# Four moves in the order of a diffusion layer: two at the opening, one in the first modulation pairs, one at the start of the second FFN

## The chip, the cores and the metric

The kernel runs on one core of a Trainium2 chip. The metric is the device time of one execution in microseconds (us). Engines are named as the profile names them: PE (matrix multiplications; PEld is its weight load), DVE (vector), ACT (activation and copies with scale), POOL, and SP, which here only issues DMA transfers. A queue of an engine is shown as SPq, POOLq and so on.

## The reference, cut to what matters

One layer, float32, on 256 latent tokens `x` and 256 context tokens `ctx`, each 2048 wide:

```python
mod_l = (silu_c @ w_mod[l] + b_mod[l]).reshape(B, N_MOD, D_MODEL)
mod_c = (silu_cc @ w_mod[l] + b_mod[l]).reshape(1, N_MOD, D_MODEL)
xl = half_step_ffn(xl, mod_l, 0, g_norm[l, 0], w_ffn1_up[l], w_ffn1_down[l])
xc = half_step_ffn(xc, mod_c, 0, g_norm[l, 0], w_ffn1_up[l], w_ffn1_down[l])
...                                   # attention and mLSTM mix both sequences
xl = half_step_ffn(xl, mod_l, 6, g_norm[l, 2], w_ffn2_up[l], w_ffn2_down[l])
```

`half_step_ffn` normalises a token by its root mean square, multiplies by `1 + scale` and adds `shift` (two of the nine rows of the modulation), multiplies by `w_up` (2048 to 2 x 5632), forms `silu(a) * b`, multiplies by `w_down` and adds the gated result. The scale and shift of the first FFN (rows 1 and 0 of `w_mod`, 2 x 16 MB) have to be computed before its first multiplication; that is the opening of the kernel. The second FFN runs on the latent tokens alone.

## The kernel before, in words

Products in float32 are made of three float32r products: each operand is split into `hi` (ACT, line 126) and `lo` (DVE, line 127). Tokens stand transposed, as 16 column blocks `k` of 128 features by 512 tokens, in `hhi` and `hlo`.

**The opening** (lines 485 to 743, about the first 128 us) does four things at once. It loads the four token tiles `xs` (context 0 and 1, latent 0 and 1, 1 MB each). It computes the conditions: `cc`, a 16 KB tensor with both condition vectors, is loaded twice (as `cc`, and as `c8` in a tile called `hi`), goes through Silu on ACT, is transposed by PE into `cP`, and is spread over the 128 partitions by 16 matmuls with 8 rows (tile `cB`, lists `spread`). It normalises the token tiles (`squares`, `factor`, `normal`) and turns them with PE, 512 columns a group (`turned`; ACT copies each group back, line 556). And it streams the first two rows of `w_mod` in 32 units of 1 MB through four buffers `mraw` (`mod_unit`), plus parts of `w_up` for the first three column pairs of the hidden layer (`products`, loads `w_pre`). `idle(n)` issues n matmuls whose result nobody reads.

The two modulation rows are computed for blocks of columns (`BLOCKS`): one column block alone, seven pairs, one alone. For a pair there are four units of `w_mod`, in this order of loading; I call them **D** (shift of the pair's first column, summed by DVE against `cB`, twice 2.3 us), **A** (shift of its second column), **B** and **C** (scale of both columns, half the rows each). A, B and C are multiplied by PE with `cP` (`mod_sums`; in the profile `tr<-mraw,cP`, because the bank has the name `tr`). Between these sums PE works off the waiting products of the pair before (`steps(prods)`: six matmuls a step for a pair). After C the sums are transposed (`mod_turned`, `tr<-ident,row`), DVE and ACT form the scaled tokens (`pair_scaled`), and the rest of the old products (18 matmuls) is issued. The four token tiles have four groups each; two of each are turned at once (`N_FIRST`), the other eight by `turned_ahead`, one at a time between the sums: three in the first pair, three in the second, two in the third.

In this stretch vector, tensor and scalar instructions are pinned to the order in which the code issues them; SP's loads too (`tc.keep_in_program_order`). Later a scheduler orders what is not pinned. SP issues its transfers one after the other; a load whose buffer is not free holds up those behind it.

**The second FFN** (from line 2030 on) streams `w_up2` and `w_dn2` in units of 1 MB through five `raw` slots (`ask` issues a load, `next_split` takes the next loaded tile, splits it and asks for one more). Its first hidden block is a plain product (`up(1)`, called through `unit`), the others are `quad`s: products on quarter matrices whose weight tiles `chain2c` and `chain2r` are summed by accumulating DMAs. The tiles of the first quad are loaded by `first_tiles`: `chain2c`, two tiles, and later `chain2r`. Five loads are asked for ahead, each plain unit asks for one more, and `first_tiles(0, ...)` stands after the second plain unit.

Of the kernel before, what the change touches and what calls it, by code (L numbers as in the profile page):

```python
# [9 lines left out]
F32 = mybir.dt.float32  # L10
# [3 lines left out]
AF = mybir.ActivationFunctionType  # L14
# [5 lines left out]
P = 128  # L20
D = 2048
# [27 lines left out]
CTX, LAT = 0, 1  # L49
# [7 lines left out]
def tile_layer(ctx: ExitStack, tc: tile.TileContext, I: dict, out: bass.AP):  # L57
    nc = tc.nc
# [12 lines left out]
    def bank():  # L71
        return ps["mm"].tile([P, 512], F32, tag="mm", name="mm")

    def tbank():
        return ps["tr"].tile([P, 512], F32, tag="tr", name="tr")
# [136 lines left out]

    sm.tile([P, 16], F32, name="smpad", bufs=1)
    cc = sm.tile([32, P], F32, tag="gr", name="cc")
    tc.keep_in_program_order(nc.sync.dma_start(cc, I["cc"]))
    nc.scalar.activation(cc, cc, AF.Silu)
    SC = cst.tile([P, 3, 2, KT], F32, name="SC")
    SH = cst.tile([P, 3, 2, KT], F32, name="SH")
    cst.tile([P, 40], F32, name="cstpad")
# [5 lines left out]
    def conditions(cB, h0, h1, seqs=(CTX, LAT)):  # L225

        for s in seqs:
            nc.sync.dma_start(cB[s], ccd[s, h0 * 1024 : h1 * 1024].partition_broadcast(P))
# [12 lines left out]
    def scale_of(n, s, kk):  # L241

        vector[0].scalar_tensor_tensor(SC[:, n, s, kk], SC[:, n, s, kk], 1.0, gnT[:, n, kk], op0=ALU.add, op1=ALU.mult)
# [48 lines left out]
    class Beside:  # L292
# [49 lines left out]
        def steps(self):  # L342
            half = None
            while self.n < len(self.items) or self.due or self.late:
                while self.n < len(self.items):
                    h = self.items[self.n][2]
                    if h != half:
                        half = h
                        conditions({LAT: self.cB}, h, h + 1, (LAT,))
                        self.waits += WAIT  # L350
                    if self.n not in self.slots or self.done < np.interp(self.n, *zip((0, 0), *self.pace)) + self.waits:
                        break
                    self.one()
                yield
                self.done += 1
                for x in [x for x in self.due if x[0] <= self.done]:
                    self.due.remove(x)
                    self.finish(*x[1:])
                if self.late and self.late[0][0] <= self.done:
                    mod_rows_out(*self.late.pop(0)[1:])  # L360
# [17 lines left out]
    def mod_rows_out(i, s, v):  # L378

        pg = tbank()  # L380
        tc.keep_in_program_order(nc.tensor.transpose(pg[:KT, :P], v, ident))
        gr = sm.tile([KT, P], F32, tag="gr", name="gr")
        nc.vector.tensor_copy(gr, pg[:KT, :P])
        nc.sync.dma_start(mod_rows[i][s, :].rearrange("(k p) -> k p", p=P), gr)
# [91 lines left out]
    xsrc = {CTX: I["ctx"], LAT: I["x"]}  # L476
# [9 lines left out]
    pre = [[bank(), bank()] for _ in range(NPRE)]  # L486
    with pool(name="st", bufs=1) as st:
        scratch.append(st)
        cP = st.tile([P, KT, 32], F32, name="cP")
        nc.gpsimd.memset(cP, 0.0)  # L490
        xs0 = {}

        vector[0], tensor[0] = Pinned(nc.vector), Pinned(nc.tensor)
        still = wp.tile([P, 1024], F32R, tag="lo", name="lo", bufs=4)[:, :CB]
# [37 lines left out]
        def squares(s, t):  # L532

            ss = sm.tile([P, 4], F32, tag="ss4", name="ss4", bufs=4)[:, :2]
            x, n = xs0[s, t], 1280
            tc.keep_in_program_order(nc.scalar.activation(junka, x[:, :n], AF.Square, accum_out=ss[:, 0:1]))
            x = x[:, n:]
            vector[0].scalar_tensor_tensor(junk[:, : D - n], x, 1.0, x, op0=ALU.mult, op1=ALU.mult, accum_out=ss[:, 1:2])
            return ss
# [11 lines left out]
        def turned(s, t, g, b):  # L551

            x = xs0[s, t][:, g * CB : (g + 1) * CB]
            for j in range(4):
                tensor[0].transpose(b[:, j * P : (j + 1) * P], x[:, j * P : (j + 1) * P], ident)
            tc.keep_in_program_order(nc.scalar.activation(x, b, AF.Copy))

        def turned_ahead():

            for g in range(N_FIRST, NCB):  # L560
                for s in (CTX, LAT):
                    for t in range(2):
                        turned(s, t, g, tbank())
                        yield

        def columns(s, k0, k1):
# [32 lines left out]
        def mod_unit():  # L599
            if ready:  # L600
                return ready.pop(0)
            raw = st.tile([P, 2048], F32, tag="mraw", name="mraw", bufs=4)
            tc.keep_in_program_order(nc.sync.dma_start(raw, I["w_m0"][next(unit)]))
            return raw

        def mod_sums(i, k0, k1, last=iter(())):

            n = (k1 - k0) * P
            nk = 2048 // n
            b = tbank()[:, :n]  # L610
            for g in range(KT // nk):
                if g == KT // nk - 1:
                    steps(last)
                raw = mod_unit()
                for j in range(nk):
                    k = nk * g + j
                    q = 32 * (j % 4)
                    tensor[0].matmul(
                        b[q : q + 32, :], cP[:, k, :], raw[:, j * n : (j + 1) * n], start=k < 4, stop=k >= KT - 4, tile_position=(0, q), skip_group_check=True
                    )  # L620
                yield
            row = st.tile([P, 256], F32, tag="row", name="row", bufs=3)[:, :n]
            scalar[0].activation(row, b, AF.Copy)
            turns.append((i, k0, k1, row))
# [15 lines left out]

        turns = []

        xs2 = [st.tile([P, 2, D], F32, name=f"xs{s}") for s in (CTX, LAT)]
        for s in (CTX, LAT):
            for t in range(2):
                x = xs0[s, t] = xs2[s][:, t, :]
                tc.keep_in_program_order(nc.sync.dma_start(x, xsrc[s][t * P : (t + 1) * P, :]))
        tc.keep_in_program_order(nc.sync.dma_start(vecs, I["vecs"]))
        ready += [mod_unit(), mod_unit()]
        prods = products(1, pre, 0, 1, hhi, hlo, True)  # L650
# [26 lines left out]
        last = squares(*tiles[3])  # L677
# [17 lines left out]
        ahead = turned_ahead()  # L695
        for k0, k1 in BLOCKS[1:]:
            kk = slice(k0, k1)
            following = products(1, pre, k0, k1, hhi, hlo, middle=True)
            if k1 - k0 == 2:
                raw = mod_unit()  # L700
            for i in range(2):
                for n, _ in enumerate(mod_sums(i, k0 if i else k1 - 1, k1, following if i else iter(()))):
                    steps(prods, 3 - (k1 - k0))
                    if not n:
                        steps(ahead)
                if i:
                    steps(ahead)
                if not i and k1 - k0 == 2:
                    for s in (CTX, LAT):
                        vector[0].scalar_tensor_tensor(  # L710
                            junk.bitcast(FP8), raw, 1.0, cB[:, s, :], op0=ALU.mult, op1=ALU.mult, accum_out=SH[:, 0, s, k0 : k0 + 1], saturate=False
                        )
                    biased(0, k0, k0 + 1)

            if k0 != 1:
                steps(following)
            mod_turned()
            if k0 != 1:
                steps(prods)
            for s in (CTX, LAT):  # L720
                scale_of(0, s, kk)
            if k0 == 1:
                steps(following)
                steps(prods)
            if k1 - k0 == 1:
                x_scaled(k0)
            else:
                for s in (CTX, LAT):
                    pair_scaled(k0, s)
            drain(prods)  # L730
            prods = following
            if k0 == 1:
                scalar[0] = nc.scalar
            if k1 == KT:
                nc.sync.dma_start(ccd.rearrange("s (k p) -> (s k) p", p=P), cc)
# [565 lines left out]
    with ExitStack() as mx:  # L1301
# [197 lines left out]
        st = states()  # L1499
# [214 lines left out]
        k1 = one([P, 2, 2, T], "k1", F32R, tag="slot1")  # L1714
# [218 lines left out]
        for cb in range(NCB):  # L1933
            bs = []
            weave(out_proj(cb, (1,), bs), xT)
            if cb == NCB - 1:

                pre = [[bank()[:, : T + 2], bank()[:, : T + 2]] for _ in range(NPRE)]
                prods = products(2, pre, 0, 4, h2hi, h2lo, both=True)
# [26 lines left out]
        for q in range(NCB):  # L1966
            if q:
                prods = products(2, pre, 4 * q, 4 * q + 4, h2hi, h2lo)
# [10 lines left out]
    with f2x:  # L1979
# [54 lines left out]
        sets = [[f3.tile([P, 2048], F32, tag=f"{g}{q}", name=f"chain2{g}{q}") for q in range(2)] for g in "cr"]  # L2034
# [57 lines left out]
        def first_tiles(ab, c, tiles):  # L2092
            for q in range(2):
                pin(nc.sync.dma_start(tiles[q], part(QUADS[0], ab, c + q)))
# [251 lines left out]
        def unit(n=1):  # L2346
            for _ in range(n):
                next(plain_units)
                clock[0] += 2
                turned()  # L2350

        ask(nc.sync, N_RAW)
        for n in range(3):
            unit()
            if n == 1:
                first_tiles(0, 0, sets[0])
                steps(forms)
        for n in QUADS:
            for step, _ in enumerate(quad(n)):
# [172 lines left out]
```

## Time and profile before

| | us |
|---|---|
| median of 3 runs | 2596.65 (2595.49 to 2597.49) |
| the profiled execution: its own time | 2592.96 |
| its span in the trace | 2591.3 |
| PE busy in the span | 2568.9 (99%) |
| DVE busy | 2167.0 (84%) |
| ACT busy | 1442.8 (56%) |

The span runs from the first to the last instruction; 1.7 us of the execution's own time lie outside it, and this execution was 3.7 us below the median. In rows of the timeline the first number is the start in us from the span's start, the second how long the group lasted from its first start to its last end; in brackets stands how long the engine was idle before it, and what ended the wait. In rows of DMA issues the last number is the time from issue to landing.

### The profile page before, as it was taken

The numbers are of one execution on the slowest core, as the hardware profiler recorded it, in microseconds if no ns is written. First come the engines' busy times: TensorE is split into PE (matmuls) and PEld (weight loads), VectorE is DVE, ScalarE is ACT, GpSimd is POOL, SyncE is SP. The second block draws the span as 40 slices with busy tenths as digits, with TensorE's granted clock in tenths as the row PEclk, the third lists the DMA queues.
The fourth block names the chain that finished last, engine by engine and source line by source line (L and its number), as shares of the span: only waits on it lengthen the run. The fifth ranks groups of instructions, "written<-read, shape, count | busy, mean of one in ns | idle before, by whom it ended". The sixth has DMA issues, their size and how long they took to land.

```text
span 2591.3 us, 33902 instructions
## 1 busy us (share of the span) xinstructions
PE 2568.9 (99%) x12659; PEld 2142.3 (83%) x12659; DVE 2167.0 (84%) x2826; ACT 1442.8 (56%) x1877; POOL 262.4 (10%) x359
## 2 busy tenths in 40 slices
PE   8999999999999999999999999999999999999998
PEld 6688888888888888888889989888897888888887
DVE  6698888878888788888887888798888888888888
ACT  5454444444444465444454457467476767666664
POOL 0000000100000100000110000110001111111111
PEclk9999999999999999999999999999999999999999
DMA  9889999999999988889986887677768899999985
GB/s 390 344 226 274 269 284 273 257 278 285 257 292 263 279 248 240 214 218 226 228 258 256 299 289 244 236 267 263 262 219 279 266 274 272 269 277 272 275 259 187
DMA packets 127669, 684.72 MB, mean 264 GB/s; under 512 B 14208, under 2 KB 16768, under 8 KB 64912
## 3 DMA queue, kind: packets, MB, share of 16 engines
q0 software_dynamic: 42048, 284.18, 46.4%
q1 hardware_dynamic: 85456, 398.37, 41.4%
q8 instruction: 99, 1.62, 0.2%
q14 instruction: 66, 0.54, 0.1%
HBM read 664.60 MB, written 17.89 MB: 263 GB/s over the span
## 4 chain that ended last, share of the span: by engine, by line
PE 93%; DVE 2%; DMA 2%; ACT 1%; issue 1%; POOL 0%; ACTq 0%; POOLq 0%; SPq 0%; DVEq 0%
PE mm L172 54%; PE Y L172 7%; PE X L172 6%; PE mm L150 4%; PE mm L149 4%; PE mm L148 4%; PE mm L85 3%; PE tr L149 2%; PE tr L150 2%; PE tr L148 2%; PE tr L85 1%; DVE lo L127 1%; DMA mraw<-in_w_m 1%; PE tr L876 1%; PE mm L1755 1%
## 5 line engine op out<-in xcount | busy, mean ns | idle before, releaser
L126 ACT ACTIVATE hi<-raw 128x1024 fp32r<-128x1024 f32 (+3 forms) x490 | 499.4, 1036 | 356.3 <-PE mm L172 220.5
L127 DVE TENSOR_TENSOR lo<-raw,hi 128x1024 fp32r<-128x1024 f32 (+2 forms) x476 | 563.6, 1204 | 150.3 <-ACT hi L126 108.7
L172 PE MATMUL mm<-hi,hhi 128*128 128x512 f32 (+3 forms) x1024 | 391.2, 384 | 0.0
L172 PE MATMUL mm<-hi,hlo 128*128 128x512 f32 (+3 forms) x1024 | 385.0, 378 | 0.0
L126 ACT ACTIVATE hi<-chain 128x1024 fp32r<-128x1024 f32 x240 | 247.5, 1056 | 223.3 <-PE mm L172 102.2
L127 DVE TENSOR_TENSOR lo<-chain,hi 128x1024 fp32r<-128x1024 f32 x240 | 287.9, 1221 | 82.5 <-ACT hi L126 74.3
L172 PE MATMUL mm<-lo,hhi 128*128 128x512 f32 (+3 forms) x1024 | 253.6, 378 | 0.0
L233 DVE SCALAR_TENSOR_TENSOR junk<-sraw,cBh 128x1024 fp8e5<-128x1024 f32 x192 | 234.4, 1221 | 17.7 <-DMA sraw<-in_w_mt 15.3
L172 PEld LDWEIGHTS mm<-hi,hhi 128*128 128x128 f32 x1024 | 192.9, 188 | 31.4
L172 PEld LDWEIGHTS mm<-hi,hlo 128*128 128x128 f32 x1024 | 192.8, 188 | 31.0
L172 PEld LDWEIGHTS mm<-lo,hhi 128*128 128x128 f32 x1024 | 187.1, 188 | 33.0
L127 DVE TENSOR_TENSOR lo<-chain2c,hi 128x1024 fp32r<-128x1024 f32 x112 | 135.6, 1222 | 34.3 <-ACT hi L126 30.1
L126 ACT ACTIVATE hi<-chain2c 128x1024 fp32r<-128x1024 f32 x112 | 118.5, 1061 | 70.6 <-PE mm L172 47.4
L127 DVE TENSOR_TENSOR lo<-chain2r,hi 128x1024 fp32r<-128x1024 f32 x104 | 125.9, 1222 | 28.4 <-ACT hi L126 24.4
L126 ACT ACTIVATE hi<-chain2r 128x1024 fp32r<-128x1024 f32 x104 | 110.4, 1061 | 63.1 <-PE mm L172 45.1
L172 PE MATMUL mm<-lo,hid2h 128*128 128x512 f32 x352 | 137.3, 390 | 0.0
L172 PE MATMUL mm<-hi,hid2l 128*128 128x512 f32 x352 | 137.0, 390 | 0.0
L172 PE MATMUL mm<-hi,hid2h 128*128 128x512 f32 x352 | 135.8, 390 | 0.0
L777 POOL DMA_DIRECT2D chain<-in_w_up1b x60 | 52.6, 877 | 732.7 <-DVE lo L127 606.7
L233 DVE SCALAR_TENSOR_TENSOR sr<-sr,cBl 128x1024 f32<-128x1024 f32 x85 | 102.5, 1217 | 15.8 <-DMA sr<-in_w_mt 15.8
L172 PE MATMUL mm<-hhi,hi 128*128 128x512 f32 (+1 forms) x256 | 83.9, 347 | 0.0
L172 PE MATMUL mm<-hlo,hi 128*128 128x512 f32 (+1 forms) x256 | 81.3, 337 | 0.0
(519 smaller groups left out, 5751.8 us busy)
## 6 DMA issues: line engine op xcount, KB each, us to landing
chain<-in_w_up1b POOLq DMA_DIRECT2D x60, 1024.0 KB, 10.5
sraw<-in_w_mt SPq DMA_DIRECT2D x96, 512.0 KB, 8.0
raw<-in_w_dn POOLq DMA_DIRECT2D x48, 1024.0 KB, 12.6
chain2c<-in_w_up2b POOLq DMA_DIRECT2D x44, 1024.0 KB, 10.9
chain2r<-in_w_up2b POOLq DMA_DIRECT2D x42, 1024.0 KB, 9.8
sr<-in_w_mt SPq DMA_DIRECT2D x82, 512.0 KB, 5.5
raw<-in_w_up1b SPq DMA_DIRECT2D x40, 1024.0 KB, 8.5
mraw<-in_w_m SPq DMA_DIRECT2D x32, 1024.0 KB, 8.1
```

The lines of the kernel that those rows point to most:

```text
L85: ins = getattr(self.engine, name)(*a, **k)
L126: scalar[0].activation(hi, src, AF.Copy)
L127: vector[0].tensor_tensor(lo, src, hi.bitcast(F32), op=ALU.subtract)
L148: tensor[0].matmul(out_ap, sh, mh, start=first, stop=False, skip_group_check=skip)
L149: tensor[0].matmul(out_ap, sh, ml, start=False, stop=False, skip_group_check=skip)
L150: tensor[0].matmul(out_ap, sl, mh, start=False, stop=last, skip_group_check=skip)
L172: tensor[0].matmul(o, st_, mv, start=first, stop=last, skip_group_check=skip)
L233: ins = nc.vector.scalar_tensor_tensor(junk() if junk else raw, raw, 1.0, cB[s], op0=ALU.mult, op1=ALU.mult, accum_out=mT[:, i, s, kt, h : ...
L777: accum = lambda dst, src: nc.gpsimd.dma_start(dst, src, accum_op=ALU.add)
L876: nc.tensor.transpose(tb[:, j * P : (j + 1) * P], ca[:, j * P : (j + 1) * P], ident)
L1755: nc.tensor.matmul(o[t][:, g * P : (g + 1) * P], av[:, k, kv * HD : (kv + 1) * HD], p[:, k * P : (k + 1) * P], start=g == 0 and k == 0, st ...
```

## The change

Four things are edited.

1. `token_load`: the load of the first context tile is issued before the two loads of `cc`; the other three token tiles and everything else on SP follow as before. (The tile pair `xs2` is therefore allocated earlier.)
2. `turned_ahead` takes two banks (`unused`) that the first pair's products have not reached yet, for the second tile of each sequence in the first group row; and in the first pair it is stepped twice where it was stepped once. The first pair turns five groups, the second three, the third none.
3. `mod_sums(..., both)`: for the six pairs from column 3 on, units B and C are multiplied one right after the other, and the two steps of products that stood after B and after C follow together.
4. `first_tiles(0, ...)` of the second FFN is called after the first plain unit instead of the second.

```diff
-    tc.keep_in_program_order(nc.sync.dma_start(cc, I["cc"]))
-    nc.scalar.activation(cc, cc, AF.Silu)
...
+        token_load(CTX, 0)
+        tc.keep_in_program_order(nc.sync.dma_start(cc, I["cc"]))
+        tc.keep_in_program_order(nc.scalar.activation(cc, cc, AF.Silu))
...
+        unused = [pre[2][1], pre[2][0]]
...
-                        turned(s, t, g, tbank())
+                        turned(s, t, g, unused.pop() if unused and (s, t) in ((CTX, 1), (LAT, 1)) else tbank())
...
-                yield
+                if g or not both:
+                    yield
...
-                for n, _ in enumerate(mod_sums(i, k0 if i else k1 - 1, k1, following if i else iter(()))):
-                    steps(prods, 3 - (k1 - k0))
+                for n, _ in enumerate(mod_sums(i, k0 if i else k1 - 1, k1, following if i else iter(()), i and 2 < k0 < k1 - 1)):
+                    steps(prods, 2 if i and 2 < k0 < k1 - 1 else 3 - (k1 - k0))
                     if not n:
-                        steps(ahead)
+                        steps(ahead, 2 if k0 == 1 else 1)
...
             unit()
+            if n == 0:
+                first_tiles(0, 0, sets[0])
             if n == 1:
-                first_tiles(0, 0, sets[0])
                 steps(forms)
```

SP at the very beginning, before; `hi<-in_cc` is the load of `c8`:

```order
L215 DMA cc<-in_cc 32x128
L508 DMA hi<-in_cc 8x512
L647 DMA xs_159<-in_ctx 128x2048 x2
L647 DMA xs_160<-in_x 128x2048 x2
L648 DMA vecs<-in_vecs 128x296
L603 DMA mraw<-in_w_m 128x2048 x2
```

and with the change:

```order
L493 DMA xs_112<-in_ctx 128x2048
L496 DMA cc<-in_cc 32x128
L514 DMA hi<-in_cc 8x512
L493 DMA xs_112<-in_ctx 128x2048
L493 DMA xs_113<-in_x 128x2048 x2
L654 DMA vecs<-in_vecs 128x296
L611 DMA mraw<-in_w_m 128x2048 x2
```

The 16 KB loads now stand behind one megabyte; the rest keeps its order.

PE in one of the middle pairs, from the products after unit A on (`tr<-mraw,cP` are units B and C), as a difference:

```order
 L85 MATMUL mm<-hlo,hi 128x512 x2
-L85 MATMUL tr<-mraw,cP 32x256 x8
+L85 MATMUL tr<-mraw,cP 32x256 x16
 L85 MATMUL mm<-hhi,hi 128x512
 L85 MATMUL mm<-hhi,lo 128x512
 L85 MATMUL mm<-hhi,hi 128x512
 L85 MATMUL mm<-hhi,lo 128x512
 L85 MATMUL mm<-hlo,hi 128x512 x2
-L85 MATMUL tr<-mraw,cP 32x256 x8
 L85 MATMUL mm<-hhi,hi 128x512
```

Unit C moves up past six product matmuls; nothing else in the pair moves. On DVE no instruction changes its place in the whole program.

SP at the start of the second FFN, before (seven plain loads, then the two chained tiles) and with the change:

```order
L2081 DMA raw<-in_w_up2b 128x2048 x7
L2094 DMA chain2c_16095<-in_w_up2b 128x2048
L2094 DMA chain2c_16096<-in_w_up2b 128x2048
L2081 DMA raw<-in_w_up2b 128x2048
L2094 DMA chain2r_16097<-in_w_up2b 128x2048
```

```order
L2087 DMA raw<-in_w_up2b 128x2048 x6
L2100 DMA chain2c_16093<-in_w_up2b 128x2048
L2100 DMA chain2c_16094<-in_w_up2b 128x2048
L2087 DMA raw<-in_w_up2b 128x2048 x2
L2100 DMA chain2r_16095<-in_w_up2b 128x2048
```

The seventh plain load changes places with the two chained tiles; POOL's own DMAs keep their order.

More of the change, by code (lines that the diff above doesn't have):

```diff
@@ L490, in tile_layer, with token_load @@
         nc.gpsimd.memset(cP, 0.0)
-        xs0 = {}
+        xs2 = [st.tile([P, 2, D], F32, name=f"xs{s}") for s in (CTX, LAT)]
+        xs0 = {(s, t): xs2[s][:, t, :] for s in (CTX, LAT) for t in range(2)}
+        def token_load(s, t):
+            tc.keep_in_program_order(nc.sync.dma_start(xs0[s, t], xsrc[s][t * P : (t + 1) * P, :]))
+        token_load(CTX, 0)
+        tc.keep_in_program_order(nc.sync.dma_start(cc, I["cc"]))
+        tc.keep_in_program_order(nc.scalar.activation(cc, cc, AF.Silu))
         vector[0], tensor[0] = Pinned(nc.vector), Pinned(nc.tensor)
@@ L604, in mod_unit, with mod_sums @@
             return raw
-        def mod_sums(i, k0, k1, last=iter(())):
+        def mod_sums(i, k0, k1, last=iter(()), both=False):
             n = (k1 - k0) * P
@@ L641, in tile_layer @@
         turns = []
[L643 to L647, printed above, removed]
+        for s, t in ((CTX, 1), (LAT, 0), (LAT, 1)):
+            token_load(s, t)
         tc.keep_in_program_order(nc.sync.dma_start(vecs, I["vecs"]))
```

## The prediction

> **What bounds the kernel now.** First the page: is one engine busy all the time?
>
> ```profile
> span 2591.3 us, 33902 instructions
> PE 2568.9 (99%) x12659; PEld 2142.3 (83%) x12659; DVE 2167.0 (84%) x2826; ACT 1442.8 (56%) x1877; POOL 262.4 (10%) x359
> ```
>
> PE is idle for 22.4 us in all, so an edit can gain little except where those idle times lie. The edits touch the opening and the start of the second FFN. The opening by windows (from:to, length, busy us of PE, PEld, DVE, ACT, POOL, then granted PE clock, DMA share, GB/s):
>
> ```profile
> 10.00:20.00 10.00, 8.98 (x42) 6.36 (x45) 8.06 (x16) 7.33 (x13) 2.20 (x4) 0.68 1.02 427
> 53.37:66.52 13.15, 13.15 (x112) 9.46 (x112) 9.25 (x18) 6.38 (x12) 0.00 (x0) 1.00 0.94 367
> 66.52:78.77 12.25, 12.25 (x104) 8.47 (x103) 9.34 (x18) 5.19 (x10) 0.00 (x0) 1.00 0.97 359
> ```
>
> Early on the DMAs set the pace (427 GB/s, PE idle 1 us in ten); the last two rows are the third and fourth pair, from unit A to the next unit A, with PE full and the DMAs nearly so. Which of the two ends the opening is told by the chain of waits (start, us, what):
>
> ```profile
> 96.29 1.04 PE tr L85 x16
> ...
> 97.36 11.93 DMA mraw<-in_w_m
> ...
> 109.33 1.07 PE tr L85 x16
> 110.40 1.59 PE mm L85 x6
> ...
> 112.32 4.14 PE mm L85 x18
> 116.46 1.01 PE tr L85 x32
> 117.47 2.94 PE mm L85 x12
> ```
>
> The chain passes through a transfer: unit C of the seventh pair landed at 109.29 and PE had waited for it. From there PE runs without a gap to 123. So this landing is the anchor of the opening, and what PE saves ahead of it is lost in the wait unless the landing moves too.
>
> **First edit: the token tile first.** SP, ACT and PE at the beginning, then landings of single issues (the tile issued at 1.66, `vecs` issued at 3.62, unit B of the first pair issued at 20.9), then the range for all units:
>
> ```profile
> 0.80 0.40 SPq L215 DMA_DIRECT2D cc<-in_cc  x1
> 1.66 0.83 SPq L647 DMA_DIRECT2D xs<-in_ctx  x2
> 2.48 0.31 ACT L216 ACTIVATE cc<-cc 32x128 f32<-32x128 f32 x1 [0.41 <-DMA cc<-in_cc]
> 3.84 0.31 PE L85 MATMUL tr<-ident,cc 32*128 32x32 f32 x1
> 4.08 2.32 PE L85 MATMUL mm<-lo 128*128 128x512 f32 x5
> 6.33 4.49 PE L85 MATMUL mm<-lo,hi 8*128 8x512 f32 x16
> xs<-in_ctx SPq DMA_DIRECT2D x1, 1024.0 KB, 4.7
> vecs<-in_vecs SPq DMA_DIRECT2D x1, 148.0 KB, 10.6
> mraw<-in_w_m SPq DMA_DIRECT2D x1, 1024.0 KB, 7.6
> DMA to landing us min/median/max: 4.8/8.1/16.1
> ```
>
> `vecs`, 148 KB, took 10.6 us because four megabytes stood ahead of it: small loads do not overtake. So `cc`, issued behind the tile, lands with it, at about 0.80 + 4.7 = 5.5, not by 2.48. Its Silu (0.31) and all of ACT, the transpose on PE and the copies on DVE queue behind it; the transpose comes at about 5.9 instead of 3.84. The five idle matmuls and the spread follow in PE's order, so the opening's PE, ACT and DVE work is S = 2.1 us late. Below: 0, if the small load did overtake (until 3.84 the idle matmuls hide 1 us). Above: 5.0, if the spread also runs at half clock (the five idle matmuls took 0.46 each, the sixteen of the spread 0.28; 16 x 0.18 = 2.9 more). I take 2.1.
>
> [...]
>
> In return the stream of megabytes starts 0.86 us sooner (0.80 for 1.66). That gain is soon spent: unit B of the first pair can be issued only when PE has multiplied the first unit, at 20.9 + 2.1 = 23.0, and lands no sooner than 4.8 later, at 27.8; before it landed at 20.9 + 7.6 = 28.5. So the stream is between 0.7 early and, from S = 2.8 on, late. I take 0 for the stream further on.
>
> **Second edit: two more groups in the first pair.** Where PE waited there:
>
> ```profile
> 28.94 1.07 PE L85 MATMUL tr<-mraw,cP 128*32 128x256 f32 x16 [0.69 <-ACT xs L556]
> 32.94 1.07 PE L85 MATMUL tr<-mraw,cP 128*32 128x256 f32 x16 [1.60 <-DMA mraw<-in_w_m]
> ```
>
> A group costs PE (13.15 - 12.25) / 2 = 0.45 us, by the pairs with two and with none. One new group lies in the wait of 0.69, the other and the 2.1 of the first edit run into the 1.60: PE leaves this place 2.1 + 0.45 - 1.6 = 1.0 late. In the second pair two groups now stand next to each other and share two banks with the transposes of the sums: I put 0.4 (between 0 and 0.8, two waits for copies of the size of the one in the first row). The third pair loses both groups: -0.9. Sum at the fourth pair: 1.0 + 0.4 - 0.9 = +0.5.
>
> **Third edit: B and C in a row.** Twelve products after C cost 2.94 (last row of the chain) instead of twice 1.59: -0.25 a pair, -1.5 for six, if PE set the pace. But C is wanted 1.6 sooner, before the six products that used to stand ahead of it. Landings of the C units of the fifth and sixth pair, issued at 72.85 and 85.1, and PE's window ahead of the seventh:
>
> ```profile
> mraw<-in_w_m SPq DMA_DIRECT2D x1, 1024.0 KB, 10.3
> mraw<-in_w_m SPq DMA_DIRECT2D x1, 1024.0 KB, 11.0
> 108.50:109.33 0.83, 0.05 (x1) 0.00 (x1) 0.83 (x2) 0.00 (x0) 0.00 (x0) 1.00 1.05 444
> ```
>
> They landed at 83.1 and 96.1, the seventh at 109.29: 13.0 apart, more than PE's 12.25. The sixth was used at 96.29, with 0.2 to spare; for the seventh PE stood still for 0.8. Moved 1.6 forward, PE stands still for it. So the third edit's 1.5, like the second's 0.9, ends at the anchor: C of the seventh pair lands when it did, and behind it come 2.94 of products instead of 1.59. The opening ends 2.94 - 1.59 = 1.35, say **+1.4 us** later. Bounds: +0.7 with the stream 0.7 ahead, +1.9 with it late by the 0.5 by which PE would free buffers later in the fourth pair.
>
> **Fourth edit: the first chained tiles.** SP, ACT and PE, the landings of the plain loads issued at 1944.99 and 1946.93, a piece of the chain and a later wait:
>
> ```profile
> 1944.99 0.42 SPq L2081 DMA_DIRECT2D raw<-in_w_up2b  x1
> 1946.93 0.33 SPq L2081 DMA_DIRECT2D raw<-in_w_up2b  x1
> 1947.31 0.42 SPq L2094 DMA_DIRECT2D chain2c<-in_w_up2b  x1
> 1958.18 2.00 ACT L126 ACTIVATE hi<-chain2c 128x1024 fp32r<-128x1024 f32 x2 [4.50 <-DMA chain2c<-in_w_up2b]
> 1958.61 0.39 PE L172 MATMUL mm<-hi,h2lo 128*128 128x512 f32 x1
> 1959.29 0.49 PE L172 MATMUL X<-hi,h2hi 128*128 128x512 f32 x1 [0.30 <-ACT hi L126]
> 1960.55 0.50 PE L172 MATMUL X<-lo,h2hi 128*128 128x512 f32 x1 [0.76 <-DVE lo L127]
> 1960.89 0.39 PE L172 MATMUL X<-hi,h2lo 128*128 128x512 f32 x1
> raw<-in_w_up2b SPq DMA_DIRECT2D x1, 1024.0 KB, 7.0
> raw<-in_w_up2b SPq DMA_DIRECT2D x1, 1024.0 KB, 8.7
> 1976.94 2.73 PE Y L172 x12
> 1991.69 0.50 PE L172 MATMUL Y<-lo,n1f 128*128 128x512 f32 x1 [0.47 <-DVE lo L127]
> ```
>
> ACT waits 4.50 us for the tile; PE loses 0.4 before X (1959.29, where 1958.61 + 0.23 was due) and 0.9 inside it (1.26 between its first two starts, 0.34 between the next). Now the tile is issued behind the sixth load, at 1945.4, and lands in the seventh's place, at 1946.93 + 8.7 = 1955.6, some 2.5 sooner than by ACT's start at 1958.18. With hi and lo (1.1 + 1.2) it is ready by 1958.0, ahead of 1958.8: both losses go, **-1.3 us**. Bounds 0 (its memory is freed late) and -1.8 (DVE, then ahead, is also on time for PE's later wait of 0.5). The seventh load, now behind the tiles, lands two transfers of 2.5 after the first tile, near 1961; its matmuls, Y, start at 1976.94. PE is full from here to the end, so a gain stays.
>
> **Sum.** +1.4 - 1.3 = +0.1 on the span of 2591.3, which lies 1.7 under its execution's 2592.96 and that 3.7 under the median; against the median, 2596.65 + 0.1 = **2596.8**.
>
> **Rivals.** *The loads keep up* (17%). If part of the holes in the stream (359 and 367 GB/s in the pairs, 427 before) came from PE freeing buffers late, C would be in time, and PE's own sum holds: +0.5 - 1.5 and the wait of about 0.8 at 109.33 gone, -1.8; with the FFN -3.1: 2593.5. For it speaks the low rate; against it, that C needs 1.6 and the sixth had 0.2.
>
> *The opening stays cold* (18%), the case on the slower side. The gap before the transpose leaves the spread at half clock, S = 5.0. Past S = 2.8 the stream pays: unit B lands at 20.9 + 5.0 + 4.8 = 30.7, 2.2 late, and every later C with it: 1.4 + 2.2 - 1.3 = +2.3: 2598.9. For it speaks the 0.68; against it, that the spread ran warm before.
>
> *The chained tile is no sooner* (10%), because its memory is still read when its turn comes: only the opening's +1.4 is left, 2598.0. Against: before, its issue followed the one ahead at once.
>
> **How the numbers follow.** My forecast has 48%, with 2595.5 to 2598.0 of its own; 7% lie outside all four. The range 2593.2 to 2599.4 takes in both outer cases. A measurement of this kernel can tell about 0.2%, 5.2 us, from no change; no case reaches that, so faster and slower come only from the 7%: 0.04 and 0.03, the same 0.93.
>
> **What would show it.** `cc`'s Silu at about 5.5 and the transpose near 5.9; PE about 1 us late behind unit C of the first pair; PE waiting for `mraw` in several pairs, and the seventh C landing at 109 to 110 with twelve products behind it; FFN1's first hidden products 1.4 later; `chain2c` split 2.5 sooner against the last plain products, and X without a gap. If PE does not wait for C, the third step is wrong; if `cc` is still there by 3, the first.

## The result, and the profile after

The changed kernel takes 2600.26 us (median of 18 executions, 2596.56 to 2606.70), the kernel before 2595.14 (18 executions, 2592.71 to 2597.94) on the same chip. The ratio is 1.0019, with a 95% interval of 1.0012 to 1.0026: 5 us slower, where 0.1 was forecast and 2599.4 was the upper end of the range. The profiled execution of the changed kernel is its longest, 2606.70.

The page of the changed kernel:

```profile
span 2605.0 us, 33902 instructions
PE 2574.7 (99%) x12659; PEld 2147.5 (82%) x12659; DVE 2167.0 (83%) x2826; ACT 1442.7 (55%) x1877; POOL 262.5 (10%) x359
```

The instructions are the same; PE is busy for 5.8 us more (the same matmuls, some at a lower clock: the mean granted was 0.997 for 0.998) and idle for 30.3 us instead of 22.4.

SP, ACT and PE at the beginning of the changed kernel (start, us, what, in brackets the wait):

```profile
1.23 0.42 SPq L496 DMA_DIRECT2D cc<-in_cc  x1
5.84 0.31 ACT L497 ACTIVATE cc<-cc 32x128 f32<-32x128 f32 x1 [3.76 <-DMA cc<-in_cc]
6.29 0.28 PE L85 MATMUL tr<-ident,cc 32*128 32x32 f32 x1 [2.38 <-ACT cc L497]
6.50 2.50 PE L85 MATMUL mm<-lo 128*128 128x512 f32 x5
8.93 7.19 PE L85 MATMUL mm<-lo,hi 8*128 8x512 f32 x16
```

`cc` came behind the megabyte, as forecast (4.6 us from issue to landing, Silu at 5.84, 5.5 was said). But the spread took 7.19 instead of 4.49: it ran cold, as at half clock, from end to end. Its matmuls took 0.63 us each; in the kernel before twelve of them, between 6.9 and 9.3 at a granted clock of 1.00, took 0.39 each, and products of as many columns in a stretch of the changed kernel at 0.50 (1480.4 to 1482.4) took 0.63. The trace of the changed kernel records the clock only from 21.69 on. Everything behind the spread on PE, ACT and DVE was 5.1 late, not 2.1.

PE's waits for `mraw` between 40 and 128 us (total, times, longest), first in the changed kernel, then in the kernel before:

```profile
PE tr L85 <- DMA mraw<-in_w_m: 5.8, 3, 2.2
```

```profile
PE tr L85 <- DMA mraw<-in_w_m: 0.8, 1, 0.8
```

The chain of waits in the changed kernel's opening, two of its rounds:

```profile
65.62 11.19 DMA mraw<-in_w_m
...
76.85 1.07 PE tr L85 x16
77.92 2.96 PE mm L85 x12
...
81.39 0.09 DVE SC L85
...
81.90 1.09 ACT hhi L598 x2
...
85.69 2.22 DVE junkv L85 x2
...
87.94 2.31 DVE junkv L85 x2
...
90.45 0.15 SPq L611
...
90.65 0.42 SPq L444
...
91.16 11.65 DMA mraw<-in_w_m
...
102.86 1.26 PE tr L85 x16
104.12 4.33 PE mm L85 x12
```

In the kernel before the chain passed through one transfer of the opening after 40 us; here it passes through three. They are the C units of the second, fourth and sixth pair; in the pairs between, C was there in time. Unit C of one pair is multiplied, its sums are transposed, DVE forms `SC` (the pair's scales), the tokens are scaled, DVE can sum unit D (`junkv`), D's buffer comes free, SP issues the load behind it (line 611), `w_pre` (line 444), and only then the next C. The last row is new: twelve products took 4.33 us, where they take 2.96 one round above. The windows around it:

```profile
100.20:103.61 3.41, 1.36 (x28) 0.54 (x20) 3.38 (x5) 1.58 (x2) 0.00 (x0) 1.00 1.01 406
103.61:107.03 3.42, 3.42 (x15) 2.40 (x8) 0.44 (x1) 0.39 (x1) 0.00 (x0) 0.50 1.00 419
107.03:110.44 3.41, 3.41 (x17) 2.78 (x17) 1.20 (x7) 0.96 (x2) 0.00 (x0) 1.00 1.01 420
```

PE was busy for 1.36 of 3.41 us, because it waited 2.05 for unit C, and then had half its clock (0.50) for just 3.41 us.

DVE's last sum of the opening, before and after (the first number is its start):

```profile
125.60 0.16 DVE L85 TENSOR_REDUCE SC<-tr 128x2 f32<-128x8 f32 x1
```

```profile
133.90 0.16 DVE L85 TENSOR_REDUCE SC<-tr 128x2 f32<-128x8 f32 x1
```

So the opening ends 8.3 us later. DVE's instructions stand in the same order in both kernels, so that the shift between the two traces can be followed: +8 until 930, +12 from 986, +15 from 1500, +13.7 behind the start of the second FFN. There the fourth edit did its work; the chain in the changed kernel has no wait left:

```profile
1957.94 16.35 PE mm L172 x72
1974.29 5.44 PE X L172 x24
1979.72 5.44 PE mm L172 x24
```

### The profile page after: what moved, and what is told of

The parts are those of the page before. It is cut to its first block, busy times and chain, and to the rows that moved or that the text cites. A ratio compares the mean times of both kernels' runs of the same rounds, so it can differ in the third digit from the quotient of the medians.

```text
span 2605.0 us, 33902 instructions
## 1 busy us (share of the span) xinstructions
PE 2574.7 (99%) x12659; PEld 2147.5 (82%) x12659; DVE 2167.0 (83%) x2826; ACT 1442.7 (55%) x1877; POOL 262.5 (10%) x359
## 4 chain that ended last, share of the span: by engine, by line
PE 89%; DVE 4%; DMA 3%; ACT 1%; issue 1%; SPq 0%; POOL 0%; ACTq 0%; POOLq 0%; DVEq 0%
PE mm L172 53%; PE Y L172 7%; PE X L172 6%; PE mm L150 4%; PE mm L148 4%; PE mm L149 4%; PE mm L85 2%; PE tr L149 2%; PE tr L150 2%; PE tr L148 2%; DMA mraw<-in_w_m 1%; DVE lo L127 1%; DMA sr<-in_w_mt 1%; DVE sr L231 1%; PE tr L882 1%
```

## The experiments

All times are against runs of the kernel before on the same chip, 11 or 12 executions to each kernel and 21 to 35 of the kernel before (18 of each in the first row); 0.1% is 2.6 us, and an interval is about 0.09% to either side. **S** is the lateness of the first sums of `mraw` (19.86 in the first profile of before), **end** that of the opening's last SC, **C waits** PE's waits for `mraw` from 40 to 128, **half** the half-clock windows of 3.41 us (granted clock 0.50) between 24 us and the end of the opening. These four come from one profile each, and the time from all executions. A difference between two rows carries both their errors, about 0.13%. A spread is called warm when it took 4.4 to 5.1 us and cold when it took 7.2 to 7.5 (the times of half clock, by the 0.63 above).

| kernel | edits | S | end | C waits | half | time, % (95%) |
|---|---|---|---|---|---|---|
| changed kernel | 1 2 3 4 | 5.1 | +8.3 | 5.8 | 1 | +0.19 (0.12, 0.26) |
| after_again | 1 2 3 4 | 4.8 | +7.2 | 5.3 | 1 | +0.15 (0.07, 0.24) |
| before_again | none | -0.2 | -0.3 | 0.5 | 0 | -0.05 (-0.13, 0.04) |
| only_first | 1 | 5.2 | +5.7 | 0 | 2 | +0.12 (0.03, 0.20) |
| only_second | 2 | 2.7 | +0.8 | 1.5 | 0 | -0.03 (-0.12, 0.06) |
| only_third | 3 | 0.1 | +2.9 | 4.0 | 0 | +0.17 (0.09, 0.26) |
| only_fourth | 4 | 2.7 | +0.4 | 0.2 | 0 | 0.00 (-0.09, 0.09) |
| second_fourth | 2 4 | -0.1 | -0.7 | 0.9 | 0 | -0.12 (-0.21, -0.04) |
| 2and4_again | 2 4 | 2.7 | +0.1 | 0.2 | 0 | -0.10 (-0.21, 0.01) |
| no_first | 2 3 4 | -0.2 | +3.2 | 4.5 | 1 | +0.10 (0.01, 0.19) |
| first_second_fourth | 1 2 4 | 5.2 | +2.2 | 0 | 0 | -0.04 (-0.13, 0.04) |
| warm | 1 2 3 4, more idle matmuls | 2.6 | +6.1 | 5.9 | 1 | +0.15 (0.06, 0.23) |
| filled_gap | 1 2 4, more idle matmuls | 2.4 | +1.4 | 1.8 | 0 | -0.10 (-0.18, -0.01) |
| cc_aside | 1 2 4, `cc` on ACT's queue | 6.8 | +4.8 | 1.4 | 0 | +0.09 (0.00, 0.18) |
| turn_early | 2 3 4, sums turned sooner | 2.7 | +4.0 | 5.0 | 0 | +0.06 (-0.03, 0.15) |
| late_turn | 2 4, sums turned later | 2.7 | +0.8 | 0.9 | 0 | -0.08 (-0.16, 0.01) |
| kept_busy | 2 4, idle matmuls near 1466 | 2.6 | +1.7 | 1.9 | 0 | -0.15 (-0.23, -0.06) |
| c_ahead_with_third | 2 3 4, C's load sooner | 2.7 | 0.0 | 1.6 | 0 | -0.19 (-0.28, -0.11) |
| c_ahead | 2 4, C's load sooner | 2.7 | 0.0 | 1.0 | 0 | -0.14 (-0.23, -0.05) |

### The edits apart

Each of these kernels is the kernel before with some of the four edits, as the change's diff has them, and the others left out.

> Kernel before with the first edit alone (token tile ahead of cc). Theory that the first edit is the whole loss (its opening stays cold, S about 5, and the lateness goes round through DVE's late D sum, SP's order and the stream): +5 to +7 against before, with the spread at 7.2 us and C of the seventh pair landing near 114. Rival, that the loss is the third edit's waiting for C: the first edit alone costs at most +2.3, since the slack of the stream takes the rest.

> The changed kernel without its first edit (cc ahead of the token tile again, the other three edits kept). Theory of the first edit: between -1.6 (only the FFN's gain is left) and -0.2 (my +1.4 for the products behind the last C, less 1.6). Rival, the third edit: +2 to +4, with PE waiting for mraw in several pairs and the seventh C still near 109.

> Kernel before with the fourth edit alone (first chained tiles a unit sooner). By my fourth step and by the changed kernel's trace (shift +15.3 to +13.7 there): -1.3 to -1.6, X without a gap. Rival, that the gain is only a part of another edit's lateness caught up there: 0.

Neither the first nor the third edit is the whole loss: both kernels are slower, by 3.1 and 2.6 us. The first edit alone ended the opening 5.7 later with no wait for `mraw`; of this, two half-clock windows take up to 3.2 (an estimate: half of PE's busy time in them, 2.92 and 3.42). Windows of that kernel:

```profile
30.25:33.66 3.41, 1.97 (x19) 0.95 (x11) 3.09 (x5) 1.66 (x4) 0.00 (x0) 1.00 1.01 401
33.66:37.07 3.41, 2.92 (x19) 1.46 (x20) 3.34 (x5) 0.61 (x2) 0.00 (x0) 0.50 1.01 428
37.07:40.49 3.42, 3.42 (x23) 1.62 (x22) 0.15 (x1) 0.63 (x2) 0.00 (x0) 0.50 0.86 302
```

The fourth edit's time, 0.00% with an interval of 2.3 us to either side, decides nothing between -1.6 and 0. Its traces do: over the start of the second FFN the shift against the kernel before falls by 1.6 us in each of the 15 profiles that have this edit, and by nothing over 0.2 in those without it (before_again, only_first, only_second, only_third).

The kernel with the fourth edit alone brought a surprise at the other end. It does not touch the beginning, and yet:

```profile
4.08 2.50 PE L85 MATMUL mm<-lo 128*128 128x512 f32 x5
6.51 7.19 PE L85 MATMUL mm<-lo,hi 8*128 8x512 f32 x16
```

Its spread ran cold too, S was 2.7, and its opening ended only 0.4 later. So a cold spread is not made by the first edit alone, and 2.7 of lateness are nearly free.

> Kernel before with the third edit alone (B and C in a row). Theory that this edit puts PE into waits for C of 1 to 2.3 us in every second pair: +1.5 at the end of the opening (my +1.4), +3.2 where one of these waits is followed by a half-clock window; total +1.5 to +3. Rival, that the second edit makes these waits: no wait over 0.8 for mraw after the first pair, opening within 0.5 of before.

> Kernel before with the second and the fourth edit. Theory that the first and third make all the loss: opening 0 to +0.5, the FFN -1.6, total -1 to -1.6. Rival, that two more groups in the first pair delay the loads of the next ones: opening +1.5 or more with waits for mraw, total 0 to +1.

The third edit alone costs +0.17%, as much as all four. PE's waits in its trace:

```profile
44.89 1.07 PE L85 MATMUL tr<-mraw,cP 128*32 128x256 f32 x16 [1.39 <-DMA mraw<-in_w_m]
...
84.84 1.07 PE L85 MATMUL tr<-mraw,cP 128*32 128x256 f32 x16 [0.55 <-DMA mraw<-in_w_m]
97.57 1.07 PE L85 MATMUL tr<-mraw,cP 128*32 128x256 f32 x16 [0.63 <-DMA mraw<-in_w_m]
110.87 1.07 PE L85 MATMUL tr<-mraw,cP 128*32 128x256 f32 x16 [1.22 <-DMA mraw<-in_w_m]
```

Five waits (a fifth of 0.20 is left out), 4.0 together, where there was one of 0.8. The second and fourth edit without the others are faster than the kernel before, by 3.1 us.

### The same kernels again

The clock grid of the expectations: within each of the first two profiles the changes of PE's granted clock lie whole multiples of 3.41 us apart (in the changed kernel at 21.69, 103.61, 107.03, 963.77 and 1479.18, in the kernel before at 6.06, 9.48 and 16.30). The repeats ask whether the cold spread and the half-clock windows come with the edits or with the execution.

> The kernel before a second time. It tells what two profiles of one kernel differ by. [...] Rival, that the cold spread and the half-clock windows belong to the edits: spread 4.5 and no half-clock window after 17 us, as in the first profile.

> The changed kernel a second time. Theory of the clock grid: the opening's loss stays between +5 and +8.5 against before, by whether PE's wait of about 2 us for a C unit takes up more than half of one window; the +7 of the middle of the program (at 964 and at 1479) is chance and mostly gone, so its time lies near 2600, +3 to +5. Rival, that the losses of the middle are carried there by the edits: they come again at the same two places.

> Second and fourth edit a second time: -2 to -3.5 again if the result repeats; rival, that the first result was chance of these executions: -1.5 or less in size, by the FFN alone.

> Kernel before with the second edit alone. If the edits simply add: second and fourth -3.2, fourth -1.6 by its trace, so -1 to -2 here, with the opening 0.7 sooner or more. Rival, my second step: 0 to +0.5, the groups only move.

The kernel before against itself gives -0.05%, within its interval. The changed kernel repeats at +0.15%. Its two losses in the middle of the program did not come again, so they belonged to the execution. The later one, at 1479, is a place where every profile shows PE waiting for `hcd`, a small tile that DVE makes (near 1466 in the kernel before; the waits are 0.70 to 3.50 us long), and in 13 of the 20 a half-clock window follows. The first profile of the kernel before waits 0.70 there and has no such window, its second one waits 2.06 and has one. PE and the windows there, in the second:

```profile
1466.03 0.60 PE L1421 MATMUL tr<-hcd,ones 8*128 8x64 f32 x2 [2.06 <-DVE hcd L1416]
```

```profile
1462.67:1466.09 3.42, 1.36 (x9) 1.07 (x7) 3.42 (x17) 2.59 (x5) 0.00 (x0) 1.00 1.00 369
1466.09:1469.50 3.41, 3.41 (x12) 2.90 (x13) 3.41 (x6) 0.33 (x1) 0.00 (x0) 0.50 0.99 380
```

Together with the spread, cold in 8 of the 13 profiles without the first edit, this is chance in one execution of the size of the effects that were to be explained: the first profile of before had luck at both places. The second edit alone is -0.03% and adds 0.3 to the end of the opening of only_fourth, which was as cold: neither a gain nor a loss that could be told. The second and fourth repeat at -0.10%.

### How late cc makes the opening

Here only these lines differ from the kernel with the edits named in the table (`warm` and `filled_gap`: the first; `cc_aside`: the others, and the same for `c8`):

```diff
-        idle(4)
+        idle(10)
...
-        tc.keep_in_program_order(nc.sync.dma_start(cc, I["cc"]))
+        tc.keep_in_program_order(nc.scalar.dma_start(cc, I["cc"]))
```

> The changed kernel with ten idle matmuls instead of four ahead of cc's transpose, so that PE has no gap of 2.4 us there. Theory that the cold clock makes the loss: the spread takes 4.5 us again, S falls from 5.1 to about 2, and the time comes back from about +5 to +0.5 to +2 against before. Rival, that cc's lateness itself (2.4 us) makes the loss, whatever the clock: +4 to +5 as in the changed kernel.

> The changed kernel without its third edit. Theory that the first edit costs by its lateness (S about 5, more than the stream's slack of some 2.7) and the third by PE's waits for C, each for itself: opening +3 to +6, as with the first edit alone (+5.6), the FFN -1.6, total +0.5 to +3 against before, that is 3 to 5 more than with the second and fourth edit alone (-3.2). Rival, that the first edit costs only together with the third: total -2 to -3.

> First, second and fourth edit, with ten idle matmuls instead of four ahead of cc's transpose: cc as late as in the changed kernel, but PE without a gap. Theory that the cold clock makes most of the first edit's lateness: S about 2.6, which the stream's slack takes (with the fourth edit alone a cold spread gave S = 2.7 and +0.4 at the end of the opening): opening 0 to +1, total -1 to -3. Rival, that cc's lateness costs in itself: as without the idle matmuls, +0.5 to +3.

> First, second and fourth edit, but cc and c8 are loaded from ACT's queue, with the token tile still first on SP's. Theory that cc is late only because it stands behind the megabyte in one queue: Silu by 3, S within 0.5 of before, opening -1 to 0, total -2.5 to -3.5. Rival, that a small load waits for the megabyte from whatever queue it comes: Silu near 5.9 and S near 5 as in the changed kernel, total +0.5 to +3.

With PE kept busy, the spread took 5 us again and S fell to 2.6 and 2.4, as expected. In `warm` this changed nothing of the time: the third edit's waits were there as before. Without the third edit, S of 5.2, 2.4 and 6.8 ended the opening 2.2, 1.4 and 4.8 later (only_first, also with 5.2, 5.7 later with its half-clock windows); and S of 2.7 by a cold spread alone 0.1 to 1.7. That bears out the 2.8 from which lateness decides only to within 1.7 us. In the times first_second_fourth stands +0.08% (2 us) above second_fourth and filled_gap 0.06% below first_second_fourth; neither can be told from nothing. That the first edit costs time is shown by only_first (+0.12%); how much of it the cold spread makes is read from the traces alone.

`cc` on ACT's queue missed its aim. ACT there:

```profile
0.80 0.41 ACTq L496 DMA_DIRECT2D cc<-in_cc  x1
...
4.13 0.31 ACT L497 ACTIVATE cc<-cc 32x128 f32<-32x128 f32 x1 [1.61 <-DMA cc<-in_cc]
4.14 0.52 ACTq L514 DMA_DIRECT2D hi<-in_cc  x1
9.00 0.63 ACT L515 ACTIVATE hi<-hi 8x512 f32<-8x512 f32 x1 [4.56 <-DMA hi<-in_cc]
```

`cc` was used at 4.13, sooner than behind the tile and later than the 3 that was expected, but its second copy was issued only behind the Silu, which waits on the same engine, and took 4.9 us for 16 KB among the megabytes. The experiment swapped one queue for another and does not show what a free queue would give.

### What the third edit costs

Two theories were left: the loop in the chain above is longer by the six products that now stand between C and the transposes of its sums, or C is merely wanted 1.6 sooner. `turn_early` (against no_first) keeps C sooner and puts six products behind the transposes again, `late_turn` (against second_fourth) does the reverse:

```diff
-                    steps(prods, 2 if i and 2 < k0 < k1 - 1 else 3 - (k1 - k0))
+                    steps(prods, 1 if i and 2 < k0 < k1 - 1 else 3 - (k1 - k0))
...
-                    steps(prods, 3 - (k1 - k0))
+                    steps(prods, 2 if i and n and 2 < k0 < k1 - 1 else 3 - (k1 - k0))
```

> Second, third and fourth edit, but only six of the twelve products stand between unit C and the transposes of its sums; the other six follow later. Theory of the loop (C's sums, transposes, D's sums on DVE, the buffer, the next loads): the transposes come as soon after C as before, the loads move 1.6 sooner together with C's use, the third edit's loss goes: opening -1 to +0.5, total near -3 as with the second and fourth edit. Rival, that the loss comes from C being wanted 1.6 sooner: waits for mraw of 1 to 2.3 us stay, opening +1.5 to +3, total 0 to +2.6.

> Second and fourth edit; unit C in its old place, but from the second pair on the transposes of its sums stand behind twelve products instead of six. Theory of the loop: each turn of it (two pairs) is 1.35 longer, PE waits for C in the later pairs, opening +2 to +3.5 above that of the second and fourth edit (-0.7), total -1 to +0.5. Rival, that only C's place counts: one 1.35 at the end of the opening, no wait for mraw over 0.8, total -2 to -1.5.

The loop theory fell. With the transposes sooner PE waits as long as in no_first (5.0 for 4.5); the longest of these waits:

```profile
111.95 1.07 PE L85 MATMUL tr<-mraw,cP 128*32 128x256 f32 x16 [1.81 <-DMA mraw<-in_w_m]
```

and with the transposes later it hardly waits (0.9), and the opening ends 0.7 to 1.5 above that of the second and fourth edit: the 1.35, once. What counts is C's place. C is the last of four loads whose first goes out when PE has multiplied unit A of the pair before. SP in no_first:

```profile
72.71 12.54 SPq L605 DMA_DIRECT2D mraw<-in_w_m  x4
85.30 0.42 SPq L446 DMA_DIRECT2D raw<-in_w_pre  x1
85.82 11.30 SPq L605 DMA_DIRECT2D mraw<-in_w_m  x4
```

The row of 72.71 is a C and the three loads of the next pair, issued from 81.07 on; its C goes out at 85.82 and lands at 97.69, that is 16.6 after the first. In before, only_third, no_first and turn_early this takes 15.0 to 17.1 (fourth to seventh pair). From unit A to the next C, PE had 16.4 us of work before (from 79.86 to 96.22, say); with the third edit 14.5 to 14.7.

The last two runs move C's load ahead of `w_pre`, with and without the third edit:

```diff
-                if g == KT // nk - 1:
-                    steps(last)
                 raw = mod_unit()
+                if g == KT // nk - 1:
+                    steps(last)
```

> Second, third and fourth edit, with unit C's load issued ahead of the 0.4 MB load (w_pre) of the next pair's products. Theory that PE's waits for C are the third edit's loss: C lands some 0.9 sooner (384 KB at 430 GB/s), in each of the three or four pairs that wait, so the opening comes 2 to 3 sooner than without it (+3.2), total -1 to +0.5 instead of +2.6. Rival, that C is held by the buffers alone or that the split of w_pre is late instead: opening +2 to +4, total +1.5 to +4.

> Second and fourth edit, with the same load order. Theory: the last waits for C (0.2 to 0.4 in three pairs) go, opening 0.3 to 0.8 sooner than with the second and fourth edit alone (-0.7 to 0), total -3 to -4. Rival, that the split of w_pre and what stands behind it on ACT is late instead: +0.5 to +1.5 against the second and fourth edit.

`w_pre` is 768 KB in a pair, twice what the expectation said. SP with the third edit, and the waits that are left:

```profile
81.81 4.91 SPq L605 DMA_DIRECT2D mraw<-in_w_m  x4
86.77 0.44 SPq L446 DMA_DIRECT2D raw<-in_w_pre  x1
93.68 4.65 SPq L605 DMA_DIRECT2D mraw<-in_w_m  x4
```

```profile
PE tr L85 <- DMA mraw<-in_w_m: 1.6, 2, 1.3
```

The C issued at 86.18 landed at 96.06, 14.2 behind the first of its four (15.6 in the fourth pair, where PE still waits 1.29, and 14.0 in the seventh). The opening ends where it did before the change, though the spread was cold, and the kernel is 0.19% (0.11 to 0.28) faster than the kernel before; against no_first, +0.10%, one load moved changed the sign. So PE's waits for C were the third edit's loss: with C's load in its old place the third edit costs 0.20 to 0.22% (no_first against 2and4_again and second_fourth), with the load moved nothing that could be told (-0.19 against -0.14). Without the third edit the move gives -0.14%, which can't be told from -0.12 and -0.10.

### The clock near 1466

```diff
             ph = tbank()
+            for _ in range(6):
+                nc.tensor.matmul(ph, hhi[:, 0, :P], hhi[:, 0, :], start=True, stop=True, skip_group_check=True)
```

> Second and fourth edit, and six idle matmuls (1.4 us) ahead of the matmul that waits for hcd near 1466 us (a few rows of the scheduled part behind it change places). Theory of the clock grid, where a window with PE busy for less than half sets the next to half clock: no half-clock window there any more, 1.7 us or more saved in the executions that have it: median 1 to 2.5 below that with the second and fourth edit (-3.2), and the times closer together. Rival, that the half-clock window there has another cause: as with the second and fourth edit.

Inconclusive. Its profile has no half-clock window there (PE waits 0.76 us for `hcd`), but neither have six of the other nineteen, the times lie no closer together (2592.2 to 2598.5, and 2589.8 to 2596.9 without the idle matmuls), and -0.15% can't be told from -0.12 and -0.10.

## Why the prediction was wrong, step by step

**What bounds the kernel.** Right: what PE loses in the opening stays lost until the end, and what was gained at the second FFN stayed gained.

**First edit.** `cc` came at 5.84 as worked out. "I take 2.1" was the wrong end of the bounds: S was 4.8 to 5.2 in each of the four profiles with this edit as it stands, 2.4 of it because the transpose came later (6.29 for 3.84) and 2.7 because the spread was cold (7.19 for 4.49). The cold spread came in all four. In the 13 profiles without this edit PE is busy from 1.83 on without a pause, and the spread was warm in five and cold in eight. An estimate tells these apart: the first recorded change of the clock, carried back in steps of 3.41. It puts an edge between 5.18 and 6.18 us in the five (6.06 in the kernel before), so that the 3.41 us ahead of it hold idle matmuls and the transpose all but from end to end, and edges at 3.58 to 4.95 and 6.99 to 8.36 in the eight. With the first edit PE stands still from 3.91 to 6.29 or later and the spread begins by 9.06: no 3.41 us of busy PE lie ahead of it. With ten idle matmuls they do, and the spread took 5 us (`warm`, `filled_gap`). That such a stretch ahead of an edge decides is the author's reading; no run moved the edges. The rival with the cold spread, for which the 0.68 of the clock between 10 and 20 us spoke, had 18%. Its price held: +2.2 for S = 5.0 was worked out, and the opening of first_second_fourth ended +2.2 (2.1 and 2.9 above the two profiles of the second and fourth edit).

**Second edit.** Behind unit C of the first pair PE was 3.9 late in the changed kernel (C began at 36.80 for 32.94) and not 1.0; with S = 5.1 for 2.1 the step's own sum gives 5.1 + 0.45 - 1.6 = 3.95. Its 0.4 for the second pair did not come, and its -0.9 for the third pair did: in 2and4_again, with S = 2.7, unit A of the third pair starts 1.5 late and that of the fourth 0.6 (54.87 and 67.09 for 53.37 and 66.52). In the times it is nothing that a run could tell.

**Third edit, the step that failed most.** "The third edit's 1.5 ... ends at the anchor: C of the seventh pair lands when it did." One wait of 1.6 was taken against one fixed landing, and its loss, 1.35, counted once; the prediction's signs speak of waits in several pairs, its sum has one. But every C is tied to PE by the buffers, 15 to 17 us behind unit A of the pair before; wanted 1.6 sooner, it was late in three to five pairs, and each wait held up the loads of the next pair too. Measured: waits of 4.0 to 4.5 in only_third and no_first instead of 0.8, and +2.9 in the opening of only_third where +1.4 was said. There the seventh C landed at 110.83, 1.5 later than the 109.29 of before, and with the 1.35 behind it that is the 2.9. In no_first it landed at 109.34, as forecast, and yet the opening ended 3.2 later: PE reached it only at about 111.3, after its wait of 2.27 for the sixth C and the half-clock window behind that. The time of the third edit alone is +4.4 (2.3 to 6.8).

**Half clock behind a wait.** No term of the sum had it. In the changed kernel PE waited for C for 2.05 of the 3.41 us from 100.20 on, and in the next 3.42, all busy, the granted clock was 0.50: up to 1.7 lost behind the wait as well (an estimate, half of the 3.42; the twelve products took 1.37 more). Four of the six profiles with C sooner and its load in the old place have such a window in the opening, none of the nine with neither the first nor the third edit.

**Fourth edit.** -1.3 forecast, -1.6 in the traces, near its bound of -1.8, which counted on DVE's wait too.

**Sum.** With the measured terms: first edit +2.2, third +2.9, a half-clock window up to +1.7, fourth -1.6, so +3.5 to +5.2, against +5.1 and +3.9 measured. The openings are read against one profile of the kernel before, whose time lies 2.2 to 4.5 below that kernel's medians, so the agreement is a rough one. The forecast was wrong by the sum of two mistakes on the same side. It also treated its rivals as one or the other: the cold opening and the waits for C came together.

## What to carry to other kernels

When a wait stands in a loop that is tied to itself by a few buffers, price it in every round and not at the last: take the time from the event that frees the first buffer to the landing that is waited for, and compare it with the work that the changed order leaves between them. Before reordering PE's work to suit a load, look whether the load itself can go ahead of its neighbours in the queue; here that turned a loss of 0.10% into a gain of 0.19%. And a single profile is one draw: the spread was cold in 8 of the 13 profiles without the first edit, and the wait for `hcd` was 0.70 us in one profile of the kernel before and 2.06, with half the clock behind it, in the other. Take two profiles before costing an edit of 2 us.

## What the runs showed of the hardware

Cut into stretches of 3.41 us along the recorded changes of PE's clock, the 20 profiles have, between 20 and 2500 us, 18 stretches at full clock in which PE was busy for 0.21 (filled_gap) to 0.49 (no_first, 1.67 us from 1466.49); behind each of them stands one with a granted clock of 0.50. Three are the changed kernel's (1.36 us busy from 100.20, 1.51 from 960.36, 1.18 from 1475.77). Of the stretches with 0.50 to 0.60 only one is followed by half the clock (0.58, 1.97 us from 30.25, in only_first); the changed kernel's from 45.59, with 1.70 us, is not. In all 18 PE stood still in a single wait, of which 1.75 to 2.68 us fell into the stretch.

The clock fell behind a busy stretch too. In the kernel before, PE was never idle from 2.65 to 16.30, and its granted clock was 1.00 from 6.06 and 0.50 from 9.48 to 16.30:

```profile
6.06:9.48 3.42, 3.42 (x16) 2.56 (x15) 1.92 (x4) 2.06 (x3) 0.00 (x0) 1.00 1.02 431
9.48:12.89 3.41, 3.41 (x9) 1.79 (x8) 3.24 (x8) 2.60 (x6) 0.56 (x2) 0.50 1.02 430
12.89:16.30 3.41, 3.41 (x14) 2.98 (x15) 3.41 (x6) 2.10 (x3) 0.54 (x1) 0.50 1.02 422
```

The stretch ahead of the fall is filled from 6.33 on by the spread's matmuls, which use 8 rows; what brought the fall no run tested.
